# Feed-forwards that multiply both parts of x in one 512-column product, and run their down projections last

## The chip, the cores and the metric

The kernel runs on one core of a Trainium2 chip. The metric is device time of one launch in microseconds (us). A core has engines that work side by side and wait for each other through semaphores: TensorE (PE, matrix products, with PEld for its weight loads), VectorE (DVE), ScalarE (ACT), GpSimd (POOL), and SyncE (SP), which issues most DMAs. Each engine takes its own instructions strictly in the order in which the program gives them.

## The reference

Three blocks run one after another on x of 256 tokens by 1024 features, in fp32. The first mixes and then runs a mixture of 16 experts, the second runs a recurrence beside an attention, and the third, twice over, a feed-forward, an attention and another feed-forward. The change touches the five dense feed-forwards:

```python
# second block (d_ff 3072), once
xn = _rmsnorm(x, ffn_norm[l]); up = xn @ w_up[l]
g_ffn = _causal_dwconv(up[..., :D_FF], ffn_conv_w[l], ffn_conv_b[l])      # 3 taps along the tokens
x = x + (jax.nn.gelu(g_ffn) * up[..., D_FF:]) @ w_down[l]
# third block (d_ff 2816), four times
g, u = jnp.split(rmsnorm(x, norm) @ w_gu, 2, axis=-1)
x = x + 0.5 * ((jax.nn.silu(g) * u) @ w_down)
...
return rmsnorm(x, final_norm)
```

`rmsnorm(x, g)` is x times the inverse root of the mean square of a token, times the gain g of a feature.

## The kernel before

x is kept transposed in SBUF (`kn.xT`: feature in the partitions, eight blocks k of 128 features, 256 tokens along the free axis). Every weight matrix is cut into **units** of 256 output columns by up to eight blocks of 128 rows. `Stream` (L66 and after) holds six slots of 16 KB a partition. A raw chunk of two units lands in one slot by DMA from SP's queue; a unit is then split into two fp32r parts, hi by an ACT copy (`prep_one`, L221, recorded at L231) and lo = raw - hi by a DVE subtraction (`settle`, L236, recorded at L240). `take` (L252) hands a unit to the products and calls `ahead` (L244), which lets ACT split the unit two places further on. So in the step of unit n, ACT gets the hi copy of unit n+2 at the step's beginning and DVE gets its lo subtraction at the step's end.

A product of a unit with x is worked out from the parts: `lin_fm` (L348) issues, for each of two halves f of the unit's columns and each block k, three matmuls of 256 columns into one accumulator: hi weights by hi x, hi weights by lo x, lo weights by hi x. All products of all stages are recorded at L321. Each accumulator is one of eight PSUM banks of 512 fp32, taken in a ring; a unit uses one bank.

`step` (L411) writes down a unit's turn in this order: the products; if a norm is still open, `settle` and one piece of the norm (`pe_step`, L525); then one slice of every evacuation that was open before (`advance`, L388); `settle`; one slice of every background job. An evacuation is a generator: of a gate and up pair p, its first slice comes one step after the up product, the next slices in the steps after that.

A feed-forward (`plan_ffn` L1200, `ffn` L1224) goes over pairs p of a gate and an up unit, in groups g of four pairs (1024 hidden features; the last group has three pairs when d_ff is 2816). The order is: all pairs of group 0, all of group 1, the four down units of group 0, all of group 2, the downs of group 1, the downs of group 2. The four down units j of a group add into four banks `acc` that are held over all groups; after the last group each is added to xT, split anew for the next stage (`Next.pair`, two blocks k at once), and squared for the next norm (`Norm.pair`).

x enters the products unnormalized, only times the gain (`xgh`, `xgl`). The norm's factor of a token (`rb`, a tile of 128x256) comes during the first steps: after the first unit's products TensorE sums the squares (`nps`), DVE and POOL take the root, and after the second unit's products TensorE spreads it and ACT copies it (`rps`, `rb` at L521). The evacuation of a pair multiplies gate and up by `rb` while it reads PSUM: in `swiglu` (L1851) two DVE instructions at L1862 and L1864, a Silu on ACT (L1865), in the next step the product of the two on POOL (L1867), in the step after that the split into `hh` on ACT (L1247) and `hl` on DVE (L1248). In `ffn_two` (L1732) a convolution lies between: DVE L1744, L1746, ACT L1749, then DVE L1754 four times and ACT L1755, then POOL L1757.

At the very end `Last.finish` (L2392) multiplies xT by the final gain (ACT, L2396, eight instructions), makes the norm's factor, and `dump` (L2430) transposes on TensorE and writes out with ACT and SP.

Of the kernel before, what the change touches and what calls it, by code (L numbers as in the profile page):

```python
# [286 lines left out]
class Kern:  # L287
# [60 lines left out]
    def lin_fm(self, w, x, ps, start=True, stop=True, fs=(0, 1), cut=None):  # L348


        wh, wl = w
        xh, xl = x
        nk = wh.shape[1]
        whole = cut is None and stop
        for k0, k1 in self.cuts(nk, cut):
            for f in fs:
                o = ps[:, f * 256:(f + 1) * 256]
                c = slice(f * P, (f + 1) * P)
                if self.fine and cut is None and f == 1 and nk == 8:
                    self.tick()  # L360
                for k in range(k0, k1):
                    self.mm(o, wh[:, k, c], xh[:, k, :], start and k == 0 and (f == fs[0] or whole), False)
                    self.mm(o, wh[:, k, c], xl[:, k, :], False, False)
                    self.mm(o, wl[:, k, c], xh[:, k, :], False, stop and k == nk - 1)

# [102 lines left out]
class Norm:  # L468
# [3 lines left out]
    def __init__(self, kn, gain=None, late=False):  # L472
        self.kn, self.gain, self.late, self.last = kn, gain, late, None
        self.acc = kn.fx.tile([P, 512], F32, name="nacc", tag="nacc", bufs=2)
        self.n = 0
        self.state = 0

    def pair(self, x2):
        kn = self.kn
        sq = self.acc if self.n == 0 else kn.fx.tile([P, 512], F32, name="nsq", tag="nsq", bufs=1)  # L480
        if self.gain is None:
            kn.SC.activation(sq, x2, AF.Square)
        else:
            for f in range(2):
                kn.SC.activation(sq[:, f * 256:(f + 1) * 256], x2[:, f * 256:(f + 1) * 256], AF.Square, scale=self.gain(2 * self.n + f))
        if self.n == 3 and self.late:
            self.last = sq
        elif self.n:
            kn.G.tensor_tensor(self.acc, self.acc, sq, op=OP.add)  # L489
        self.n += 1  # L490

    def mean(self):
        kn = self.kn
        ps = kn.psB("nps")
        for t in range(2):
# [29 lines left out]
    def pe_step(self):  # L525
        if self.state == 0:
            self.columns()
        elif self.state == 1:
            self.rows()
            self.kn.norm = None  # L530
        self.state += 1
# [8 lines left out]


# [50 lines left out]

class Next:


    def __init__(self, kn, gain, norm=None, at=None):
        self.kn, self.gain = kn, gain
        self.hi, self.lo = (kn.act("xgh"), kn.act("xgl")) if at is None else (at[:, 0], at[:, 1])
        self.norm = norm or Norm(kn)

    def pair(self, j):
        kn = self.kn
        for k in (2 * j, 2 * j + 1):
            kn.split(self.hi[:, k, :], self.lo[:, k, :], kn.xT[:, k, :], self.gain(k))
        self.norm.pair(flat(kn.xT[:, 2 * j:2 * j + 2, :]))

# [617 lines left out]
def ffn(kn, plan, nx, gated, add, nxt, lend=0):  # L1224
# [4 lines left out]
    follow = None  # L1229
    for it in plan["order"]:  # L1230
        if it[0] in ("gate", "up"):
            _, p, u = it
            g, q = divmod(p, 4)
            ps = kn.psB(it[0])
            w = st.take(u)
            if it[0] == "gate":
                cur["g"] = ps
                kn.step(lambda: kn.lin_fm(w, nx.x, ps, cut=(2, 4, 6) if p == 0 else None))
            else:
                if q == 0:  # L1240
                    hs[g] = (kn.act("hh"), kn.act("hl")) if g != 1 else (kn.act2("hh"), kn.act2("hl"))

                def evac(p=p, q=q, g=g, pg=cur["g"], pu=ps):
                    o = slice(2 * q, 2 * q + 2)
                    t = yield from gated(p, pg, pu)
                    yield
                    kn.SC.activation(hs[g][0][:, o, :], t, AF.Copy)  # L1247
                    kn.V.tensor_tensor(hs[g][1][:, o, :], t, hs[g][0][:, o, :], op=OP.subtract)  # L1248
                kn.step(lambda: kn.lin_fm(w, nx.x, ps), evac)
        else:  # L1250
            _, g, j, u = it
            if g == last - 1 and j == 0:
                st.slots -= lend
            if acc is None:
                acc = [kn.psA("acc") for _ in range(4)]
            if g == last and j == 0:
                kn.flush()
                follow = nxt()
            w = st.take(u)
            n = sizes[g]  # L1260
            x = (hs[g][0][:, :n], hs[g][1][:, :n])

            def evac(j=j):
                add(j, acc[j])
                follow.pair(j)
            kn.step(lambda: kn.lin_fm(w, x, acc[j], start=g == 0, stop=g == last), evac if g == last else None, now=g == last and j == 3)
# [94 lines left out]
def mixer_two(kn, nx):  # L1361
# [3 lines left out]
    with ExitStack() as ctx:  # L1365
# [347 lines left out]
        follow = Next(kn, lambda k: kn.col("ffn_norm_2", k))  # L1713
# [18 lines left out]
def ffn_two(kn, nx):  # L1732
    V, SC, G = kn.V, kn.SC, kn.G
    with ExitStack() as ctx:
        kn.open_act2(ctx)
        pool = ctx.enter_context(kn.pool("ffn2"))
        kn.norm = nx.norm
        p3 = lambda ps: ps.rearrange("p (a b) -> p a b", a=2)

        def gated(p, pg, pu):  # L1740
            rb2 = nx.norm.rb2
            g = pool.tile([P, 2, 258], F32, name="g", tag="g", bufs=2)
            V.memset(g[:, :, 0:2], 0.0)
            V.tensor_tensor(g[:, :, 2:258], p3(pg), rb2, op=OP.mult)  # L1744
            tu = pool.tile([P, 2, S], F32, name="tu", tag="tu", bufs=3)
            V.tensor_tensor(tu, p3(pu), rb2, op=OP.mult)  # L1746
# [13 lines left out]
        def add(j, ps):  # L1760
            o = flat(kn.xT[:, 2 * j:2 * j + 2, :])
            V.tensor_tensor(o, ps, o, op=OP.add)

        return ffn(kn, kn.ffn2, nx, gated, add, lambda: Next(kn, lambda k: kn.col("ple_norm_2", k)))
# [86 lines left out]
def swiglu(kn, plan, nx, nxt, lend=0):  # L1851
    V, SC, G = kn.V, kn.SC, kn.G
    with ExitStack() as ctx:
        kn.open_act2(ctx)
        pool = ctx.enter_context(kn.pool("ffn3"))
        kn.norm = nx.norm
        p3 = lambda ps: ps.rearrange("p (a b) -> p a b", a=2)

        def gated(p, pg, pu):
            rb2 = nx.norm.rb2  # L1860
            t = pool.tile([P, 2, S], F32, name="t", tag="t", bufs=3)
            V.tensor_tensor(t, p3(pg), rb2, op=OP.mult)  # L1862
            tu = pool.tile([P, 2, S], F32, name="tu", tag="tu", bufs=3)
            V.tensor_tensor(tu, p3(pu), rb2, op=OP.mult)  # L1864
            SC.activation(t, t, AF.Silu)  # L1865
            yield
# [3 lines left out]
        def add(j, ps):  # L1870
            o = flat(kn.xT[:, 2 * j:2 * j + 2, :])
            V.scalar_tensor_tensor(o, ps, 0.5, o, op0=OP.mult, op1=OP.add)

        return ffn(kn, plan, nx, gated, add, nxt, lend)


def mixer_three(kn, nx, i):
# [4 lines left out]
    with ExitStack() as ctx:  # L1882
# [464 lines left out]
        for j in range(4):  # L2347
            until("out", 2 * j + 2)
            if j == 3:
                follow = Next(kn, lambda k: kn.col("ffn2_norm_3", 8 * i + k))  # L2350
# [30 lines left out]
class Last:  # L2381


    def __init__(self, kn):
        self.kn = kn
        self.norm = Norm(kn, late=True)
# [4 lines left out]

    def finish(self):  # L2392
# [5 lines left out]
        dump(kn, self.norm.rc)  # L2398


def block_three(kn, nx):
    for i in range(2):
        nx = swiglu(kn, kn.u3["f1", i], nx, lambda: Next(kn, lambda k: kn.col("mix_norm_3", 8 * i + k)), 1 - i)
# [3 lines left out]
                    (lambda: Next(kn, lambda k: kn.col("ffn1_norm_3", 8 + k))) if i == 0 else (lambda: Last(kn)))  # L2407
# [22 lines left out]
def dump(kn, rc=None):  # L2430

    kn.V.tensor_copy(kn.xT[:, 0, 0:1], kn.xT[:, 0, 0:1])
    with kn.pool("dump") as pool:
        o = kn.out.rearrange("b (t p) d -> p (b t) d", p=P)
        y = pool.tile([P, 2, D], F32, name="yo")
        for t in range(2):
            for q in range(2):
# [3 lines left out]
                if rc is None:  # L2441
                    kn.SC.activation(y[:, t, q * 512:(q + 1) * 512], ps, AF.Copy)
                else:
                    kn.SC.activation(y[:, t, q * 512:(q + 1) * 512], ps, AF.Copy, scale=rc[:, t:t + 1])
# [3 lines left out]
def build(tc, A, out, stages=(1, "e", 2, 3)):  # L2448
    with ExitStack() as ctx:
# [27 lines left out]
        if 2 in stages:  # L2477
# [44 lines left out]
```

## Time and profile before

| | us |
|---|---|
| median of 3 runs (2717.88 to 2722.27) | 2720.84 |
| the profiled execution's own time | 2721.21 |
| its span, first to last instruction | 2719.4 |
| PE busy in the span, 17617 matmuls | 2300.4 (85%) |
| DVE busy | 1130.3 (42%) |
| ACT busy | 911.1 (34%) |
| POOL busy | 355.4 (13%) |
| mean granted TensorE clock | 0.927 of full |

The profiled execution lies 0.37 us above the median. Shares are means over very different stages: the first 1340 us or so hold the first block and its experts and the recurrence, and the five feed-forwards lie in the second half of the span. Times below count from the span's start. A matmul's duration in a row is longer than the distance to the next one, as matmuls overlap in TensorE's pipeline: what it costs in a stream is the distance between starts. An idle time in square brackets is that of the engine before this instruction, with what ended it.

### The profile page before, as it was taken

To read this page: it belongs to the slowest core of one execution; us is meant where nothing else is said; L and a number is where in the kernel's file an instruction comes from. 1 tells how busy PE (TensorE), PEld (TensorE's weight loads), DVE (VectorE), ACT (ScalarE), POOL (GpSimd) and SP (SyncE) were. 2 spreads that over 40 slices of the span, in tenths; PEclk is the share of its full clock that TensorE was granted. 3 is DMA by queue.
4 is the path that set the end of the run, shared out by engine and by line. 5 is a ranking of instruction groups with operands and counts; after the bars stand their busy time and mean duration, and the time that the engine had idled before them with its cause. 6 is when DMAs were issued, how large, how long until landed. Compare 5 with 4: busy or idle time off the path is not lost. (4 is left out here: it accounts for less than half of the span.)

```text
span 2719.4 us, 39924 instructions
## 1 busy us (share of the span) xinstructions
PE 2300.4 (85%) x17617; PEld 1836.1 (68%) x17617; DVE 1130.3 (42%) x1325; ACT 911.1 (34%) x1223; POOL 355.4 (13%) x223
## 2 busy tenths in 40 slices
PE   7998766555566556589899999999999999998999
PEld 5987221111121111169899999999979999997998
DVE  5445000000000000049866666555686555558653
ACT  4343000000000000036845545434555444445533
POOL 0001000000000000002301212212322222130211
PEclk8998887887888787889999999999999999999999
DMA  8688999999999999984346555555335555562651
GB/s 325 232 279 346 389 428 427 428 428 428 428 428 428 428 427 428 428 301 152 132 155 221 186 186 171 186 179 177 94 96 185 187 192 175 180 173 78 201 186 63
DMA packets 266258, 717.92 MB, mean 264 GB/s; under 512 B 10995, under 2 KB 190436, under 8 KB 238436
## 3 DMA queue, kind: packets, MB, share of 16 engines
q1 hardware_dynamic: 262252, 710.38, 69.2%
q10 hardware_dynamic: 3000, 3.02, 0.5%
q8 instruction: 138, 2.26, 0.3%
q0 software_dynamic: 832, 1.97, 0.3%
q14 instruction: 36, 0.29, 0.0%
HBM read 713.89 MB, written 1.44 MB: 263 GB/s over the span
## 5 line engine op out<-in xcount | busy, mean ns | idle before, releaser
L240 DVE TENSOR_TENSOR w<-raw,w 128x2048 fp32r<-128x2048 f32 (+1 forms) x273 | 617.3, 2264 | 261.3 <-ACT w L231 261.2
L231 ACT ACTIVATE w<-raw 128x2048 fp32r<-128x2048 f32 (+1 forms) x273 | 510.9, 1875 | 568.5 <-PE up L321 137.7
L321 PE MATMUL gu<-raw,xe 128*32 128x512 f32 x1360 | 236.8, 833 | 175.9 <-DMA raw<-in_w_gate_e_dram 89.3
L321 PE MATMUL gate<-xgh,w 128*128 128x256 f32 x1792 | 329.0, 282 | 0.0
L321 PE MATMUL up<-xgh,w 128*128 128x256 f32 x1792 | 328.9, 282 | 0.0
L321 PE MATMUL acc<-hh,w 128*128 128x256 f32 x1792 | 320.6, 281 | 0.0
L321 PEld LDWEIGHTS gu<-raw,xe 128*32 128x32 f32 x1360 | 45.6, 132 | 362.9 <-issue 137.9
L321 PEld LDWEIGHTS up<-xgh,w 128*128 128x128 f32 x1792 | 278.9, 188 | 0.3 <-DVE w L240 0.2
L321 PEld LDWEIGHTS gate<-xgh,w 128*128 128x128 f32 x1792 | 278.9, 188 | 0.0
L321 PEld LDWEIGHTS acc<-hh,w 128*128 128x128 f32 x1792 | 275.6, 188 | 0.0
L321 PE MATMUL gate<-xgl,w 128*128 128x256 f32 x896 | 253.1, 282 | 4.4 <-DVE xgl L339 4.3
L1162 DVE TENSOR_TENSOR sg<-sg,gu 128x512 f32<-128x512 f32 x16 | 11.0, 688 | 583.3 <-PE gu L321 583.3
L321 PE MATMUL acc<-hl,w 128*128 128x256 f32 x896 | 252.1, 281 | 0.0
L321 PE MATMUL up<-xgl,w 128*128 128x256 f32 x896 | 252.1, 281 | 0.0
L1867 POOL TENSOR_TENSOR t<-t,tu 128x512 f32<-128x512 f32 x44 | 130.4, 2964 | 452.6 <-ACT t L1865 448.1
L321 PE MATMUL gu<-rawx,xe 128*32 128x512 f32 x688 | 109.0, 763 | 77.3 <-DMA rawx<-in_w_up_e_dram 41.2
L321 PEld LDWEIGHTS gate<-xgl,w 128*128 128x128 f32 x896 | 168.7, 188 | 5.9 <-DVE xgl L339 5.9
L321 PEld LDWEIGHTS acc<-hl,w 128*128 128x128 f32 x896 | 168.7, 188 | 0.0
L321 PEld LDWEIGHTS up<-xgl,w 128*128 128x128 f32 x896 | 168.7, 188 | 0.0
L321 PE MATMUL py<-raw,hT 128*32 128x512 f32 x672 | 93.5, 689 | 59.5 <-DMA raw<-in_w_down_e_dram 51.4
L321 PEld LDWEIGHTS gu<-rawx,xe 128*32 128x32 f32 x688 | 21.5, 124 | 168.2 <-issue 53.2
L1170 ACT ACTIVATE hT<-ph 128x512 f32<-128x512 f32 x16 | 9.6, 597 | 359.1 <-PE ph L1168 359.1
(441 smaller groups left out, 3366.9 us busy)
## 6 DMA issues: line engine op xcount, KB each, us to landing
raw<-in_w_up_e_dram SPq DMA_DIRECT2D x44, 2048.0 KB, 39.1
raw<-in_ffn_w_gu_dram SPq DMA_DIRECT2D x88, 1024.0 KB, 6.6
raw<-in_w_down_e_dram SPq DMA_DIRECT2D x42, 2048.0 KB, 39.1
raw<-in_w_gate_e_dram SPq DMA_DIRECT2D x41, 2048.0 KB, 39.1
rawx<-in_w_gate_e_dram SPq DMA_DIRECT2D x23, 2048.0 KB, 39.1
rawx<-in_w_down_e_dram SPq DMA_DIRECT2D x22, 2048.0 KB, 39.1
rawx<-in_w_up_e_dram SPq DMA_DIRECT2D x20, 2048.0 KB, 39.1
raw<-in_w_in_dram SPq DMA_DIRECT2D x32, 1024.0 KB, 9.1
```

The lines of the kernel that those rows point to most:

```text
L231: kn.nc.scalar.activation(wh, v, AF.Copy)
L240: self.kn.nc.vector.tensor_tensor(wl, v, wh, op=OP.subtract)
L321: self.nc.tensor.matmul(out, lhsT, rhs, start=start, stop=stop, skip_group_check=True)
L1162: V.tensor_tensor(sg, sg, pu, op=OP.mult)
L1170: SC.activation(flat(hT), ph, AF.Copy)
L1867: G.tensor_tensor(t, t, tu, op=OP.mult)
```

## The change

1. **One product for both parts.** x's parts lie side by side in tiles of four blocks (`Parts`), so that hi and lo of a block are one operand of two strips of 256 columns. `lin_both` replaces `lin_fm` in the feed-forwards: per f and k one matmul of 512 columns (hi weights by hi x and lo x, into the two halves of a bank) and one of 256 (lo weights by hi x, into the first half). A half f of a unit now fills a bank of its own.
2. **The halves are summed at evacuation.** `join` sums the two halves of each bank with a DVE tensor_reduce over pairs that lie 256 apart.
3. **x is scaled by the norm as well.** A background job `Scaled` makes, in four slices, a second pair of parts of x that holds gain and `rb`; pairs from p = 4 on use it and skip the multiplication by `rb`. Pairs 0 to 3 use the unscaled x as before, and multiply by `rb` in SBUF after `join`.
4. **Downs behind all gates and ups**, j by j over the groups, with two accumulator banks for one j; each j is added to xT when its last group is done, and the last unit is split into its two halves, each followed by its own addition, split and square.
5. **Norms.** `fold=True` sums the squares to 256 columns before TensorE sees them (half the `nps` matmuls) and makes the norm begin one step later; `wants` leaves out the unused `rps` and `rb` of the attentions' norms.
6. **The end.** The final gain becomes a diagonal matrix in a TensorE product that also transposes; DVE and ACT share the output's evacuation, and it is written in four DMAs on two queues.

```diff
+    def join(self, out, pss):
+        for f, ps in enumerate(pss):
+            self.V.tensor_reduce(out[:, f, :], ps.rearrange("p (h s) -> p s h", h=2), axis=AX.X, op=OP.add)
+    def lin_both(self, w, x, ps, start=True, stop=True, fs=(0, 1), cut=None):
...
+        for k0, k1 in self.cuts(nk, cut):
+            for f in fs:
+                o = ps[f].rearrange("p (h s) -> p h s", h=2)
+                c = slice(f * P, (f + 1) * P)
+                for k in range(k0, k1):
+                    self.mm(o, wh[:, k, c], x.both(k), start and k == 0, False)
+                    self.mm(o[:, 0, :], wl[:, k, c], x.hi[:, k, :], False, stop and k == nk - 1)
 class Norm:
-        self.state = 0
+        self.state = -1 if fold else 0
...
     def plan_ffn:
-    ups(0)
-    for g in range(1, len(sizes)):
+    for g in range(len(sizes)):
         ups(g)
-        downs(g - 1)
-    downs(len(sizes) - 1)
+    for j in range(4):
+        for g in range(len(sizes)):
+            order.append(("down", g, j, st.linear(ph, Wd, 8 * g, sizes[g], j * 256)))
+class Scaled:
+    def run(self, kn, nx, pool):
+        while not hasattr(nx.norm, "rb"):
+            yield
+        for q in range(4):
+            tmp = pool.tile([P, 2, S], F32, name="xs", tag="xs", bufs=2)
+            for f in range(2):
+                k = 2 * q + f
+                kn.V.scalar_tensor_tensor(tmp[:, f, :], kn.xT[:, k, :], nx.gain(k), nx.norm.rb, op0=OP.mult, op1=OP.mult)
+            o = slice(2 * q, 2 * q + 2)
+            kn.SC.activation(self.parts.hi[:, o, :], tmp, AF.Copy)
+            yield
+            kn.V.tensor_tensor(self.parts.lo[:, o, :], tmp, self.parts.hi[:, o, :], op=OP.subtract)
+        self.ready = 1
 def ffn(...):
+            x = nx.parts if p < 4 else xs.parts
+            ps = [kn.psB(it[0]) for _ in range(2)]
...
+            def half(f):
+                kn.lin_both(w, hs[g], acc, start=False, fs=(f,))
+                if f == 0:
+                    kn.advance(len(kn.late))
+                    st.settle()
+                add(6 + f, acc[f])
+                follow.part(6 + f)
 def swiglu: gated(p, pg, pu, scaled):
             t = pool.tile([P, 2, S], F32, name="t", tag="t", bufs=3)
-            V.tensor_tensor(t, p3(pg), rb2, op=OP.mult)
+            kn.join(t, pg)
+            if not scaled:
+                V.tensor_tensor(t, t, nx.norm.rb2, op=OP.mult)
+            SC.activation(t, t, AF.Silu)
-            V.tensor_tensor(tu, p3(pu), rb2, op=OP.mult)
-            SC.activation(t, t, AF.Silu)
+            kn.join(tu, pu)
+            if not scaled:
+                V.tensor_tensor(tu, tu, nx.norm.rb2, op=OP.mult)
 class Last: finish
-        for k in range(8):
-            kn.SC.activation(kn.xT[:, k, :], kn.xT[:, k, :], AF.Copy, scale=kn.col("final_norm_3", k))
+            kn.mm(pss[q, t][:, (k % 4) * P:(k % 4 + 1) * P], kn.xT[:, k, t * P:(t + 1) * P], self.diag[:, k, :], True, True)
```

`ffn_two` gets the same treatment: join gate, join up, then the two multiplications by `rb` for p below 4, then the convolution as before.

## Rows read from the trace of the kernel before

**Rows 1.** Windows, the feed-forwards: stretch, length, engines' busy time (instructions), granted clock, DMA share, GB/s
```profile
1450.18:1657.01 206.83, 206.83 (x1747) 206.83 (x1745) 130.38 (x145) 103.99 (x111) 38.97 (x18) 1.00 0.54 180
...
2516.49:2707.24 190.75, 190.10 (x1598) 189.53 (x1597) 101.07 (x77) 80.00 (x66) 42.04 (x17) 1.00 0.46 153
sum 971.28, PE 966.78 PEld 964.84 DVE 545.29 ACT 436.56 POOL 206.40; mean PE 193.36 PEld 192.97 DVE 109.06 ACT 87.31 POOL 41.28
```

**Rows 2.** Page, costliest groups: shape, count, busy us, mean ns, idle before
```profile
L321 PE MATMUL gate<-xgh,w 128*128 128x256 f32 x1792 | 329.0, 282 | 0.0
L321 PE MATMUL gate<-xgl,w 128*128 128x256 f32 x896 | 253.1, 282 | 4.4 <-DVE xgl L339 4.3
```

**Rows 3.** Timeline of PE in a down unit: start us, us, engine, line, op
```profile
1800.28 0.28 PE L321 MATMUL acc<-hl,w 128*128 128x256 f32 x1
...
1803.84 0.28 PE L321 MATMUL acc<-hl,w 128*128 128x256 f32 x1
```

**Rows 4.** Timeline of PE where 512 and 256 columns alternate, an attention
```profile
2001.47 0.28 PE L321 MATMUL S<-mask,identr 128*128 128x256 f32 x1
...
2001.59 0.63 PE L321 MATMUL S<-keys,QS 128*128 128x512 f32 x2
...
2002.05 0.28 PE L321 MATMUL S<-mask,identr 128*128 128x256 f32 x1
```

**Rows 5.** Timeline of PE, six matmuls of 512 columns in a row, first block
```profile
59.56 1.55 PE L321 MATMUL tps<-csr,uf 128*128 128x512 f32 x6
60.95 0.28 PE L321 MATMUL psA<-hh,w 128*128 128x256 f32 x1
```

**Rows 6.** Timeline of DVE around one evacuation, third block
```profile
2194.86 0.69 DVE L1248 TENSOR_TENSOR hl<-t,hh 128x512 fp32r<-128x512 f32 x1 [2.92 <-ACT hh L1247]
2195.47 0.69 DVE L1862 TENSOR_TENSOR t<-gate,rb 128x512 f32<-128x512 f32 x1
2196.07 0.68 DVE L1864 TENSOR_TENSOR tu<-up,rb 128x512 f32<-128x512 f32 x1
2196.66 2.28 DVE L240 TENSOR_TENSOR w<-raw,w 128x2048 fp32r<-128x2048 f32 x1
...
2221.41 0.89 DVE L339 SCALAR_TENSOR_TENSOR xgl<-xT,PT,xgh 128x256 fp32r<-128x256 f32 x2 [1.27 <-ACT xgh L338]
```

**Rows 7.** Timeline of ACT around the same evacuation
```profile
2192.39 1.92 ACT L231 ACTIVATE w<-raw 128x2048 fp32r<-128x2048 f32 x1 [2.78 <-PE up L321]
2194.21 0.61 ACT L1247 ACTIVATE hh<-t 128x512 fp32r<-128x512 f32 x1
2196.18 0.64 ACT L1865 ACTIVATE t<-t 128x512 f32<-128x512 f32 x1 [1.36 <-DVE t L1862]
```

**Rows 8.** Groups of DVE by shape, 1686 to 2708 us: a reduction from PSUM
```profile
L2193 DVE TENSOR_REDUCE nm<-S 128x2 f32<-128x512 f32 x16 | 10.3, 681 | 1.6 <-PE S L321 1.6
```

**Rows 9.** Timeline of DVE in the second block's feed-forward
```profile
1467.55 1.92 DVE L1754 SCALAR_TENSOR_TENSOR t<-g,PT,t 128x256 f32<-128x256 f32 x4
```

**Rows 10.** Timelines of PE and ACT: a norm's sums, and the copy of rb
```profile
2237.99 1.05 PE L321 MATMUL nps<-ones,nacc 128*128 128x1 f32 x8
...
1463.11 0.39 ACT L521 ACTIVATE rb<-rps 128x256 f32<-128x256 f32 x1 [5.12 <-PE rps L321]
```

**Rows 11.** Timeline of PE, a long wait in an attention
```profile
1898.70 0.58 PE L321 MATMUL un<-w,xgh 128*128 128x256 f32 x1 [3.80 <-DVE w L240]
```

**Rows 12.** Windows in the attentions: after waits of 3.8, 2 and 4.2 us; clock behind the counts
```profile
1898.28:1901.69 3.41, 2.99 (x14) 2.99 (x15) 2.79 (x4) 1.94 (x2) 0.95 (x1) 0.50 0.00 0
...
1940.20:1942.00 1.80, 1.80 (x15) 1.80 (x16) 1.77 (x3) 1.80 (x2) 0.00 (x0) 1.00 0.35 59
...
2461.48:2468.31 6.83, 4.38 (x19) 4.00 (x20) 6.22 (x17) 2.52 (x10) 0.00 (x0) 0.50 0.00 0
```

**Rows 13.** Timeline of the end, 2704 to 2720 us
```profile
2708.76 3.29 ACT L2396 ACTIVATE xT<-xT,PT 128x256 f32<-128x256 f32 x8
...
2710.82 3.52 PE L2440 MATMUL ops<-ident,xT 128*128 128x128 f32 x16 [0.42 <-DVE xT L2432]
```

More of the change, by code (lines that the diff above doesn't have):

```diff
@@ L494, in mean @@
         ps = kn.psB("nps")
+        if self.fold:
+            for i, a in enumerate((self.acc, self.last) if self.late else (self.acc,)):
+                for t in range(2):
+                    kn.mm(ps[:, t:t + 1], a[:, t * P:(t + 1) * P], kn.ones[:, 0:1], i == 0 and t == 0, i == self.late)
+            return ps[:, 0:2]
         for t in range(2):
@@ L527, in pe_step @@
             self.columns()
+            if "r" not in self.wants:
+                self.kn.norm = None
         elif self.state == 1:
@@ L538 @@
 class TwoNorms(Norm):
+    wants = "cr"
     def __init__(self, kn, g1, sums):
@@ L590, in rows, with __init__, __getitem__, both @@
         kn.bgs.append(scale())
+class Part:
+    def __init__(self, tiles, n, h):
+        self.tiles, self.n, self.h = tiles, n, h
+    def __getitem__(self, at):
+        p, k, c = at
+        if isinstance(k, slice):
+            k0, m = k.start, k.stop - k.start
+            return self.tiles[k0 // self.n][p, self.h, k0 % self.n:k0 % self.n + m, c]
+        return self.tiles[k // self.n][p, self.h, k % self.n, c]
+class Parts:
+    def __init__(self, kn, act, name, m=2):
+        self.n = 4
+        self.tiles = [a(name).rearrange("p (h k) s -> p h k s", h=2) for a in (act if isinstance(act, tuple) else (act,) * m)]
+        self.hi, self.lo = (Part(self.tiles, 4, h) for h in range(2))
+    def both(self, k):
+        return self.tiles[k // 4][:, :, k % 4, :]
 class Next:
@@ L605, in pair, with part @@
         self.norm.pair(flat(kn.xT[:, 2 * j:2 * j + 2, :]))
+    def part(self, k):
+        kn = self.kn
+        kn.split(self.hi[:, k, :], self.lo[:, k, :], kn.xT[:, k, :], self.gain(k))
+        if self.norm.fold:
+            self.norm.part(kn.xT[:, k, :], k % 2)
+        elif k % 2:
+            self.norm.pair(flat(kn.xT[:, k - 1:k + 1, :]))
     @property
@@ L1229, in ffn @@
     follow = None
+    xs = Scaled(kn, nx, pool)
+    kn.bgs.append(xs.gen)
     for it in plan["order"]:
@@ L1233, in ffn @@
             g, q = divmod(p, 4)
-            ps = kn.psB(it[0])
+            if p == 4 and it[0] == "gate":
+                kn.drain(xs.gen)
+                assert xs.ready
+            x = nx.parts if p < 4 else xs.parts
+            ps = [kn.psB(it[0]) for _ in range(2)]
             w = st.take(u)
@@ L1258, in ffn, with evac @@
                 follow = nxt()
+            if g == 0:
+                acc = [kn.psA("acc") for _ in range(2)]
             w = st.take(u)
[L1260 to L1264, printed above, removed]
+            def evac(j=j, acc=acc):
+                for f in range(2):
+                    add(2 * j + f, acc[f])
                 follow.pair(j)
-            kn.step(lambda: kn.lin_fm(w, x, acc[j], start=g == 0, stop=g == last), evac if g == last else None, now=g == last and j == 3)
+            def half(f):
+                kn.lin_both(w, hs[g], acc, start=False, fs=(f,))
+                if f == 0:
+                    kn.advance(len(kn.late))
+                    st.settle()
+                add(6 + f, acc[f])
+                follow.part(6 + f)
+            if g == last and j == 3:
+                kn.step(lambda: [half(f) for f in range(2)])
+            else:
+                kn.step(lambda: kn.lin_both(w, hs[g], acc, start=g == 0, stop=g == last), evac if g == last else None)
     kn.flush()
@@ L2385, in __init__ @@
         self.kn = kn
-        self.norm = Norm(kn, late=True)
+        self.norm = Norm(kn, late=True, fold=True)
+        self.diag = kn.act("diag", F32).rearrange("p a s -> p (a s)")[:, 0:8 * P].rearrange("p (k n) -> p k n", k=8)
+        for k in range(8):
+            kn.SC.activation(self.diag[:, k, :], kn.ident, AF.Copy, scale=kn.col("final_norm_3", k))
     def pair(self, j):
@@ L2390, in pair, with part @@
         self.norm.pair(flat(kn.xT[:, 2 * j:2 * j + 2, :]))
+    def part(self, k):
+        self.norm.part(self.kn.xT[:, k, :], k % 2)
     def finish(self):
```

132 lines of the change are left out of this document (86 added, 46 removed).

## The prediction, on record before the result

> **What bounds the kernel now.** I read the windows of the five feed-forwards first, then the groups of PE, then the timelines of DVE and ACT. In the windows the reader is to see that TensorE is busy in 967 of 971 us at full clock, while DVE works 545 and ACT 437, and that the DMA engines are about half busy [rows 1]. So the feed-forwards go at TensorE's rate, and a product of three matmuls is the thing to price. Gate, up and acc have 1792 + 896 matmuls each [rows 2], three names: 8064 matmuls, 2688 triples. Ten triples take 1803.84 - 1800.28 = 3.56 us [rows 3], 356 ns each, 118.7 ns a matmul; a unit of 16 triples takes 5.70 us.
>
> **The product.** A triple of 3 x 256 columns becomes a 512 and a 256: the same 768 columns, two instructions. Where 512s and 256s alternate, the 256 takes 0.12 us and two 512s take 2002.05 - 2001.59 = 0.46, 230 ns each [rows 4]; six 512s in a row take 1.39, 232 each [rows 5]. I take 231 + 119 = 350: 6 ns less for a triple, 2688 x 6 = **-16 us**. Bounds: the two strips of the operand might cost as two matmuls (356, no gain); if all above 256 columns at 2.4 GHz (106.7 ns) were a price per instruction, 12 ns, the 512 would take 225 and the gain be 32. I stay with the rows that show a 512.
>
> The Trainium skill (TensorE: Matmul & The Clock Gate, "Back-to-back issue gap") has a rule that speaks against the change: a warm matmul costs its columns at 2.4 GHz plus about 2.5 ns. By it a joined instruction would give 2.5 ns, 2688 x 2.5 = 7 us, and the forecast would be 9 us higher. The rows disagree with its level (119 where it has 109, 231 where it has 216), but agree that columns, not instructions, are most of the price.
>
> **What DVE and ACT get in the first four pairs.** This is where I see the price. Prices, start to start in a full queue, from [rows 6]: `hl` 0.6, a multiplication by `rb` 0.6, lo of a weight unit 2.2, a 256-column scalar_tensor_tensor 0.4. From [rows 7]: hi of a weight unit 1.9, `hh` 0.6. A reduction of 128x512 from PSUM takes 0.68 [rows 8] like the multiplication beside it, so 0.6 in a queue, and a `join` of one unit 1.2; no row shows pairs that lie 256 apart, so bounds: 0.6 (256 outputs as a 256-wide instruction) and 2.4 for a unit, taken 1.2, the same elements read. Evacuating a pair costs DVE 1.2 + 0.6 + 1.2 + 0.6 = 3.6 for p below 4 where it was 1.2, and 2.4 after. A slice of `Scaled` costs 0.8 on DVE, 0.6 on ACT, then 0.6 on DVE in the next step.
>
> Only order matters now. In a step ACT's queue has hi of unit n+2, then evacuation, then Scaled's hi; DVE's has evacuation, lo of n+2, then Scaled. But Scaled's hi waits for DVE's last instruction of its step, and the next step's weight hi stands behind it; DVE's lo waits for that hi, and before it `hl` waits for `hh`, which stands behind the hi too. The two engines take turns instead of overlapping. I follow a `swiglu` from its first matmul, unit = 16 x 350 = 5.6 us:
>
> - `fold` opens the norm one step later: `nps` after unit 1, `rps` after unit 2. Unit 2 ends at 3 x 5.6 + 0.45 = 17.2; with `rps` (some 0.4, an estimate) and the copy of 0.39 [rows 10] `rb` is there at 18.0. DVE has joined gate 0 and stands at the multiplication. Then 0.6 + 1.2 + 0.6 + 0.8 (Scaled 0) = 21.2.
> - Step 3: Scaled's hi 0.6, weight hi 1.9, weight lo 2.2, Scaled 1.4: 27.3.
> - Step 4: 0.6, 1.9, `hh` 0.6, `hl` 0.6, evacuation 3.6, weight lo 2.2: 36.8 is when unit 6 can start; TensorE was ready at 6 x 5.6 + 0.8 = 34.4. Then Scaled 1.4: 38.2.
> - Step 5: 6.1: 44.3.
> - Step 6: 0.6 + 1.9 + 0.6 + 0.6 + 3.6 + 2.2 = 9.5: lo of unit 8 at 53.8; TensorE was ready at 8 x 5.6 + 0.8 = 45.6.
>
> So a `swiglu` loses 8.2 us by its ninth unit, 2.4 before unit 6 and nearly all the rest before unit 8, x 4 = **+33**. From p = 4 on, an evacuation step has 0.3 + 1.9 + 0.6 + 0.6 + 2.4 + 2.2 = 8.0 us before its lo is done, of 11.2 until it is wanted: no wait. Bounds of a `swiglu`: nothing, since DVE's own work in that chain is 24.6 us of the 27.6 between `rb` and unit 8; and 8.2 + 6 with joins of 2.4 (five joins of a unit lie behind `rb`).
>
> In `ffn_two` both joins stand ahead of the multiplications, so less is left when `rb` comes, and the convolution (four of 0.4 [rows 9]) falls into the steps without a join. Followed the same way: `rb` 18.0; two multiplications and Scaled 0, 20.1; step 3, weight hi behind Scaled's and lo: 25.0, Scaled 26.4; step 4, evacuation 3.6 and lo: 32.2, Scaled 33.6; step 5, Scaled's hi, weight hi, `hh`, `hl`, convolution 1.6, lo: 41.2 against 40.0 when unit 7 is wanted; Scaled and the split of `pT`, 43.2; step 6, evacuation and lo 49.1, step 7 `xl` 49.7. Unit 8 waits till then, against 45.6: **+3.5**; with joins of 2.4 about 14.
>
> **The clock.** Unit 8 of a `swiglu` comes after 5 us of idle. In an attention TensorE waited 3.80 us [rows 11], and the granted clock was 0.50 from 1898.28 to 1901.69, with 2.99 us of matmuls in it; around 2461.48 another long wait has 6.83 us at 0.50 with 4.38 of matmuls; after a wait of 2 us the clock stayed 1.00 [rows 12]. Half of such matmul time is lost, 1.5 to 2.2; I take 2 x 4 = **+8**, bounds 0 and 14.
>
> **The rest.** Five folded norms issue 4 for 8 `nps` (1.05 us for 8, [rows 10]): -2.5; two attentions' `rps` and `rb` go, some -0.5. **-3**, bounds 0 and -5. The end loses ACT's scaling of xT 3.29 (partly behind the norm) and, of the 16 transposes 3.52 that lay on the path [rows 13], all but what now runs while the root is taken: **-2.5**, bounds 0 and -5. The downs' move keeps instructions and bytes; SP issues loads of 256 instead of 512 columns for some of them, hidden by DMA engines that are half idle [rows 1], and if that cover went, a late unit would cost TensorE its own wait, which I put at 0 to +5. Four additions where one was (0.69 to 4 x 0.4 for a j) fall on steps of down units where DVE has no evacuation. POOL's queue loses some norm work; ACT's `diag` (eight small copies) lies in down steps.
>
> **Sum**, against the profiled execution's own 2721.2 (2719.4 of span and 1.8 around it): 2721.2 - 16 - 3 - 2.5 + 33 + 3.5 + 8 = 2744.2. That execution is 0.4 above the median; I say **2744**.
>
> **Rivals.**
> 1. *The queues keep up.* Then nothing but the gains is left: 2721.2 - 21.5 = 2700. For it: DVE is busy 56% and ACT 45% of the feed-forwards now, and the lo is made two units ahead. Against it: the ping-pong needs no full engine, only order, and it is in both queues' order. It decides at 27.6 us for the chain; I count 35.8. Chance 0.20.
> 2. *The pair sums are slow*, 2.4 for a unit: 14.2 x 4 + 14 in place of 33 + 3.5, 2744 + 34 = 2778. For it: an access pattern that no row shows; against: every row of DVE from PSUM goes by elements. Chance 0.10.
> 3. *Instructions, not columns, cost*: gain 32, chain about 3 longer over the five: 2744 - 16 + 3 = 2731. Against: [rows 4, 5]. Chance 0.07.
> 4. *Half of each wait is absorbed* (weight units a little further ahead, no clock loss), so that gain and loss cancel: about 2721. Chance 0.06.
>
> The forecast has 0.57, with its own range 2725 to 2768. Fewer instructions that save nothing would be its upper part, 2760.
>
> **The numbers.** A measurement of this kernel tells a change from none at about 0.2%, 5.4 us. Faster: rival 1 and part of 4, 0.22. Within: 0.05. Slower: 0.73. The range holds the forecast, rival 1 to its lower third and rival 2: 2696 to 2780.
>
> **What will show it.** Waits of PE before unit 6 and unit 8 of each `swiglu`, ended by DVE's lo of a weight unit, with DVE waiting for ACT's hi just before, and stretches at 0.50 clock behind them; 2688 matmuls of 512 columns at a distance of some 231 ns; no waits in the pairs from p = 4 on and in the downs. If TensorE runs through units 2 to 8 with no gap, the chain is wrong and rival 1 is right; if joins last over 1 us each, rival 2; if a triple is under 345 ns, rival 3.

## The result, and the profile after

The changed kernel takes 2767.34 us (median of 4 runs, 2763.51 to 2769.80) against 2720.17 for the kernel before on the same chip (4 runs, 2717.88 to 2722.27): ratio 1.0171, 95% interval 1.0159 to 1.0183. It is slower by 47 us; 24 were forecast. The profiled execution took 2763.51, with a span of 2761.7, so the traces differ by 42.3 in span.

Windows over the same five feed-forwards as [rows 1], kernel after (stretch, length, busy time of PE, PEld, DVE, ACT, POOL with their instructions, granted clock, DMA share, GB/s):

```profile
1446.70:1658.69 211.99, 205.87 (x1167) 180.05 (x1166) 161.09 (x201) 106.91 (x117) 42.54 (x20) 0.99 0.54 175
1689.87:1892.92 203.05, 191.06 (x1064) 165.95 (x1065) 147.53 (x142) 88.19 (x82) 45.12 (x19) 0.98 0.51 167
2054.15:2256.48 202.33, 192.02 (x1066) 166.60 (x1065) 137.72 (x135) 88.04 (x78) 44.31 (x20) 0.97 0.54 174
2256.48:2455.52 199.04, 190.16 (x1067) 166.08 (x1066) 132.38 (x135) 83.93 (x74) 40.39 (x16) 0.98 0.54 172
2550.42:2752.64 202.22, 191.60 (x1067) 166.01 (x1066) 139.48 (x130) 84.70 (x80) 43.58 (x21) 0.97 0.45 144
sum 1018.63, PE 970.71 PEld 844.68 DVE 718.20 ACT 451.78 POOL 215.94; mean PE 194.14 PEld 168.94 DVE 143.64 ACT 90.36 POOL 43.19
```

The five lengths sum to 1018.6 where they were 971.3: +47.4, more than the 42.3 by which the spans differ (the table near the end has the rest). TensorE idled 4.5 us in them before and 47.9 now, and the clock is below 1.00 in all five, where it was 1.00. After the last product the end is shorter: 2752.64 to 2761.7, 9.1 us, against 12.2 between [rows 1] and the span before.

Is the product itself cheaper? The page's groups that answer to [rows 2], and the timeline of PE that answers to [rows 3] (start us, us, engine, line, op), the third `swiglu`:

```profile
L327 PE MATMUL acc<-h,w 128*128 128x512 f32 (+1 forms) x1792 | 315.7, 339 | 2.1 <-DVE h L1364 2.1
L327 PE MATMUL gate<-xn,w 128*128 128x512 f32 (+1 forms) x1152 | 218.5, 348 | 22.9 <-DVE w L240 22.3
```

```profile
2285.46 5.78 PE L327 MATMUL up<-xg,w 128*128 128x512 f32 x32
2291.07 0.39 PE L327 MATMUL gate<-xg,w 128*128 128x512 f32 x1
2295.30 4.96 PE L327 MATMUL gate<-xg,w 128*128 128x256 f32 x18 [3.84 <-DVE w L240]
```

It is: a unit of 32 matmuls goes from 2285.46 to 2291.07, 5.61 us, 351 ns a pair against 356 a triple. The last row is the cost: unit 6 has one matmul, and then TensorE waits 3.84 us for DVE's lo of a weight unit. DVE ahead of it, and ahead of unit 8 (answering to [rows 6]):

```profile
2274.84 0.69 DVE L1989 TENSOR_TENSOR t<-t,rb 128x512 f32<-128x512 f32 x1 [1.48 <-ACT rb L564]
...
2277.38 1.92 DVE L1325 SCALAR_TENSOR_TENSOR xs<-xT,PT,rb 128x256 f32<-128x256 f32 x2
2281.79 2.29 DVE L240 TENSOR_TENSOR w<-raw,w 128x2048 fp32r<-128x2048 f32 x1 [2.50 <-ACT w L231]
2284.00 0.69 DVE L1329 TENSOR_TENSOR xn<-xs,xn 128x512 fp32r<-128x512 f32 x1
2284.61 0.87 DVE L1325 SCALAR_TENSOR_TENSOR xs<-xT,PT,rb 128x256 f32<-128x256 f32 x2
2288.50 0.69 DVE L1364 TENSOR_TENSOR h<-t,h 128x512 fp32r<-128x512 f32 x1 [3.02 <-ACT h L1363]
...
2292.96 2.29 DVE L240 TENSOR_TENSOR w<-raw,w 128x2048 fp32r<-128x2048 f32 x1
2295.16 1.78 DVE L1329 TENSOR_TENSOR xn<-xs,xn 128x512 fp32r<-128x512 f32 x1
...
2300.22 2.29 DVE L240 TENSOR_TENSOR w<-raw,w 128x2048 fp32r<-128x2048 f32 x1 [2.49 <-ACT w L231]
...
2311.39 2.29 DVE L240 TENSOR_TENSOR w<-raw,w 128x2048 fp32r<-128x2048 f32 x1
```

And ACT over the same time (answering to [rows 7]):

```profile
2274.43 0.38 ACT L564 ACTIVATE rb<-rps 128x256 f32<-128x256 f32 x1 [4.59 <-PE rps L327]
...
2279.32 0.63 ACT L1327 ACTIVATE xn<-xs 128x512 fp32r<-128x512 f32 x1 [3.12 <-DVE xs L1325]
2279.86 1.90 ACT L231 ACTIVATE w<-raw 128x2048 fp32r<-128x2048 f32 x1
2285.51 0.63 ACT L1327 ACTIVATE xn<-xs 128x512 fp32r<-128x512 f32 x1 [3.75 <-DVE xs L1325]
2286.05 1.90 ACT L231 ACTIVATE w<-raw 128x2048 fp32r<-128x2048 f32 x1
2287.85 0.61 ACT L1363 ACTIVATE h<-t 128x512 fp32r<-128x512 f32 x1
```

Read them together. DVE ends `xs`; ACT, which waited 3.12 us for it, copies it (`xn`, 2279.32) and only then makes the weight's hi; DVE, which waited 2.50 us for that hi, makes the lo and the next `xs`; ACT waited 3.75 for that. Each engine is idle while the other works: the turn-taking of the forecast, with its waits in the places it named. Windows at the two late units' restarts show the clock (the third number from the right is the granted clock: 0.50, the level of 1.2 GHz):

```profile
2296.51:2299.92 3.41, 3.41 (x13) 2.93 (x12) 1.22 (x3) 2.16 (x2) 0.00 (x0) 0.50 0.00 0
2313.57:2316.99 3.42, 3.26 (x10) 2.88 (x11) 3.42 (x3) 2.43 (x2) 1.24 (x1) 0.50 0.00 0
```

Each `swiglu` has two half-speed stretches, beside TensorE's waits for units 6 and 8. Most last 3.4 us; the one at unit 8 lasts 6.8 in the second and the last `swiglu` (2112.15 to 2119.01, 2607.12 to 2613.95). `ffn_two` has one of 3.4, from 1497.8, beside a wait of 2.41 us for its unit 8.

### The profile page after: what moved, and what is told of

It reads as the page before. It is cut to its first block, busy times and chain, and to the rows that moved or that the text cites. A ratio compares the mean times of both kernels' runs of the same rounds, so it can differ in the third digit from the quotient of the medians.

```text
span 2761.7 us, 34925 instructions
## 1 busy us (share of the span) xinstructions
PE 2301.3 (83%) x14909; PEld 1712.6 (62%) x14909; DVE 1300.4 (47%) x1598; ACT 920.1 (33%) x1245; POOL 355.4 (13%) x235
## 3 DMA queue, kind: packets, MB, share of 16 engines
q8 instruction: 117, 1.92, 0.3%
## 4 chain that ended last, share of the span: by engine, by line
PE 37%; DVE 8%; ACT 3%; issue 2%; ACTq 0%; POOL 0%; DVEq 0%; POOLq 0%
PE acc L327 11%; PE gate L327 9%; PE up L327 8%; PE psA L327 3%; DVE w L240 3%; PE un L327 2%; ACT w L231 2%; PE wo L327 1%; DVE xs L1325 1%; DVE tu L319 1%; PE po L327 1%; DVE xg L345 1%; DVE xn L1329 1%; DVE t L319 0%; PE S L327 0%
## 5 line engine op out<-in xcount | busy, mean ns | idle before, releaser
L327 PE MATMUL acc<-h,w 128*128 128x512 f32 (+1 forms) x1792 | 315.7, 339 | 2.1 <-DVE h L1364 2.1
L327 PEld LDWEIGHTS acc<-h,w 128*128 128x128 f32 x1792 | 276.1, 188 | 40.8 <-DVE h L1364 2.4
L327 PE MATMUL gate<-xn,w 128*128 128x512 f32 (+1 forms) x1152 | 218.5, 348 | 22.9 <-DVE w L240 22.3
L327 PEld LDWEIGHTS gate<-xn,w 128*128 128x128 f32 x1152 | 184.3, 196 | 51.9 <-DVE w L240 24.5
L327 PE MATMUL up<-xn,w 128*128 128x512 f32 (+1 forms) x1152 | 208.1, 339 | 0.0
L327 PEld LDWEIGHTS up<-xn,w 128*128 128x128 f32 x1152 | 177.5, 188 | 24.8
L327 PE MATMUL gate<-xg,w 128*128 128x512 f32 (+1 forms) x640 | 125.4, 353 | 21.2 <-DVE w L240 15.3
L327 PE MATMUL psA<-xg,w 128*128 128x256 f32 x1104 | 141.4, 289 | 1.3 <-DVE w L240 0.8
L327 PEld LDWEIGHTS psA<-xg,w 128*128 128x128 f32 x1104 | 137.2, 193 | 3.3 <-issue 1.9
L327 PE MATMUL up<-xg,w 128*128 128x512 f32 (+1 forms) x640 | 117.5, 340 | 3.0 <-DVE w L240 3.0
```

The costliest lines, as they stand in the source:

```text
L327: self.nc.tensor.matmul(out, lhsT, rhs, start=start, stop=stop, skip_group_check=True)
```

## The experiments

All times below are medians against the kernel before on the same chip: 2718.67 us beside the first four runs, 2719.73 beside the next four, 2719.12 beside the last two. A difference from the kernel after is one between such sets, whose kernel before moved by up to 1.5 us.

### No scaled x

```
-    xs = Scaled(kn, nx, pool)
-    kn.bgs.append(xs.gen)
-            x = nx.parts if p < 4 else xs.parts
+            x = nx.parts
-                    t = yield from gated(p, pg, pu, p >= 4)
+                    t = yield from gated(p, pg, pu, False)
```

> The changed kernel without Scaled: all pairs use the unscaled x and multiply by rb in SBUF. Theory (ACT and DVE take turns because Scaled's slices stand between the weight units): the waits before units 6 and 8 of each feed-forward go, with the half clock behind them; the trace of the changed kernel has 12.8 us of them in a swiglu (units 6 to 8 take 11.24 + 6.06 + 12.32 instead of 3 x 5.62) and about 6.5 in ffn_two, so 2767 - 4 x 12.8 - 6 = 2710 (2703 to 2722), below the kernel before. Rival (DVE has too much to do altogether, for the doubled evacuation): DVE does 1.2 us more for each later pair, so the waits only spread over the later pairs, 2745 or more. Rival (the norm that comes a step later is the cause): a wait stays before units 6 and 8, 2730 or more.

Measured: 2735.12 us, ratio 1.0060 (1.0047 to 1.0072). The waits before units 6 and 8 are gone, and 32 us with them, but 25 more were expected. Windows of the first and the third `swiglu`, the waits of PE in the first (us in total, times, longest), and ACT's timeline in each:

```profile
1683.32:1887.31 203.99, 191.09 (x1065) 164.45 (x1066) 151.70 (x144) 85.43 (x78) 45.03 (x19) 0.99 0.51 166
...
2239.63:2426.96 187.33, 186.53 (x1067) 163.34 (x1065) 134.14 (x137) 81.87 (x70) 40.39 (x16) 1.00 0.57 182
```

```profile
PE gate L327 <- DVE w L240: 6.4, 7, 1.0
```

```profile
1749.20 1.92 ACT L231 ACTIVATE w<-raw 128x2048 fp32r<-128x2048 f32 x1 [4.97 <-DVE w L240]
...
1761.74 1.92 ACT L231 ACTIVATE w<-raw 128x2048 fp32r<-128x2048 f32 x1 [4.99 <-DVE w L240]
...
2294.96 3.85 ACT L231 ACTIVATE w<-raw 128x2048 fp32r<-128x2048 f32 x2 [3.55 <-DVE w L240]
...
2306.19 3.86 ACT L231 ACTIVATE w<-raw 128x2048 fp32r<-128x2048 f32 x2 [3.55 <-DVE w L240]
```

The same work settles in one of two rhythms. In the third `swiglu` a round takes 2306.19 - 2294.96 = 11.23 us, TensorE's own time for two units; in the first, 1761.74 - 1749.20 = 12.54, and TensorE waits at each gate. DVE and POOL in a slow round of the first `swiglu`, then in a fast one of the second:

```profile
1743.59 5.57 DVE L240 TENSOR_TENSOR w<-raw,w 128x2048 fp32r<-128x2048 f32 x2
1743.84 3.17 POOL L1991 TENSOR_TENSOR t<-t,tu 128x512 f32<-128x512 f32 x1 [9.36 <-DVE tu L1989]
...
2116.47 2.28 DVE L240 TENSOR_TENSOR w<-raw,w 128x2048 fp32r<-128x2048 f32 x1
2116.73 3.20 POOL L1991 TENSOR_TENSOR t<-t,tu 128x512 f32<-128x512 f32 x1 [8.05 <-DVE tu L1989]
```

In the slow rhythm DVE makes two lo right behind each other beside POOL's product and takes 5.57 us, where 2.2 + 2.3 = 4.5 would do: 1.1 of the 1.3 us by which the rounds differ (what POOL does to DVE comes below, with the product on DVE). In the fast one DVE waits for ACT between the two, and POOL is done by then. So multiplying every pair by `rb` costs too, once DVE and ACT stand in the wrong order; the expectation had priced only amounts. What makes a feed-forward fall into one rhythm or the other I did not trace.

### The copy one step later

`Scaled` issues the same instructions, but ACT's copy of a slice comes one step after its `xs`, and DVE's lo one step after that, so nobody waits within a step.

```
-        for q in range(4):
-            ...                           (xs of slice q)
-            kn.SC.activation(self.parts.hi[:, o, :], tmp, AF.Copy)
-            yield
-            kn.V.tensor_tensor(self.parts.lo[:, o, :], tmp, ...)
+        tmps = {}
+        for i in range(6):
+            if i >= 2:
+                ...                       (o, two blocks of slice i - 2)
+                kn.V.tensor_tensor(self.parts.lo[:, o, :], tmps[i - 2], ...)
+            if 1 <= i < 5:
+                kn.SC.activation(self.parts.hi[:, 2 * i - 2:2 * i, :], tmps[i - 1], AF.Copy)
+            if i < 4:
+                ...                       (xs of slice i, as before)
+            if i < 5:
+                yield
```

> The changed kernel with Scaled's work unchanged, but each slice's ACT copy given one step later, so that it stands behind the next weight unit's hi instead of ahead of it; its DVE subtraction comes another step later. Theory (order, not amount): the wait before unit 6 goes and unit 8 waits only for Scaled's last subtraction, 1 to 6 us in place of 9.4 and with at most one stretch at half clock: 2767 - 4 x 6 to 4 x 10 = 2727 to 2743. Rival (amount of DVE work in the first four pairs): the same instructions on the same engines, 2760 to 2770.

Measured: 2734.53 us, 1.0059 (1.0045 to 1.0072). Equal work in another order is 33 us faster, so order, not amount, made most of the loss. The wait before unit 6 goes; unit 8 is still late, now because its slice of x is made last (in the first and the last `swiglu` the lo of a weight unit is late by 2.2 us as well, and `ffn_two` waits 5.4 us for x). PE's waits in the third `swiglu`:

```profile
PE gate L327 <- DVE xn L1325: 2.5, 2, 2.4
```

### The norms unfolded

```
-  Norm(kn, wants="r", fold=True)
+  Norm(kn, wants="r")            (ahead of all five feed-forwards)
```

> The changed kernel with the five feed-forward norms not folded: 8 nps matmuls again, and the norm begins a step earlier, so that rb is there about 6 us earlier in units. Theory: the chain of Scaled's turns is as long, but starts earlier; followed through the queues it loses 4 us less in a swiglu and the wait before unit 8 shrinks to 1 to 2 us, which also saves one stretch at half clock: 2767 - 4 x (4 + 1.7) + 2.2 = 2746 (2735 to 2755). Rival (the late norm is the whole cause): no wait left, 2715. Rival (amount of DVE work): the work is the same but has one step more, a small gain, 2755 to 2765.

Measured: 2744.14 us, 1.0093 (1.0080 to 1.0107): 23 us faster than the kernel after. `rb` comes one step earlier, the chain starts earlier. The fold, which I priced at a gain of 2.5, cost 23 here.

### The 512 columns given as two strips

```
-                    self.mm(o, wh[:, k, c], x.both(k), start and k == 0, False)
+                    self.mm(o[:, 0, :], wh[:, k, c], x.hi[:, k, :], start and k == 0, False)
+                    self.mm(o[:, 1, :], wh[:, k, c], x.lo[:, k, :], False, False)
```

> The changed kernel with each 512-column product given as its two strips of 256 columns, all else as it is: prices the joined product by itself. The changed kernel has 175.6 ns a matmul in pairs of 512 and 256 (351 ns a pair) against 356 for three of 256 before, 4.8 ns x 2688 = 13 us. Theory: 2767 + 13, less some 3 us as the waits shrink with longer units: 2777 (2772 to 2782). Rival (joining saves nothing, the lower distance comes from elsewhere): 2767.

Measured: 2777.88 us, 1.0216 (1.0202 to 1.0230), 10.5 above the kernel after: the joined product does gain, by about the 12.5 us that its shorter distance is worth.

### Both re-timings together

The later copy and the unfolded norms in one kernel.

> Both re-timings in one kernel: Scaled's copy and low part each one step later, and the five norms ahead of the feed-forwards unfolded, so that rb is there a step earlier. All the products are as in the kernel after. Theory (order: the scaled x is late because its start waits for rb and each of its links waits for a turn of the other engine): the wait before unit 8, about 10 to 12 us where 5.6 would do in the run with the later copy alone, goes, and with it its half-clock stretch: four swiglu stretches shorter by 4 to 5 us, ffn_two by about 5, against 2 for the separate root and columns: 2712 (2704 to 2722). Rival (amount: DVE can't do joined evacuation, weights and Scaled in the time of eight units): the late unit stays and the time is that of the later copy alone, 2734, or the two gains overlap and it is over 2728.

Measured: 2710.27 us, 0.9971 (0.9961 to 0.9982): 0.3% faster than the kernel before, with every product and pair sum of the changed kernel in it. The two gains add: 33 + 23 = 56 of 57. Windows of the first and third `swiglu`, and the sum over all five feed-forwards:

```profile
1687.80:1880.55 192.75, 187.99 (x1068) 163.82 (x1069) 146.38 (x142) 88.13 (x81) 47.51 (x17) 1.00 0.54 176
...
2231.35:2418.07 186.72, 186.72 (x1071) 163.81 (x1070) 132.66 (x135) 83.66 (x73) 42.05 (x15) 1.00 0.57 183
sum 964.93, PE 954.25 PEld 834.10 DVE 716.67 ACT 450.69 POOL 223.06; mean PE 190.85 PEld 166.82 DVE 143.33 ACT 90.14 POOL 44.61
```

In the third, TensorE is busy in all of its 186.72 us while DVE does the same 133 us of work as in the kernel after. DVE and ACT where the copy and lo now stand:

```profile
2266.29 0.89 DVE L1332 SCALAR_TENSOR_TENSOR xs<-xT,PT,rb 128x256 f32<-128x256 f32 x2
2267.09 2.29 DVE L240 TENSOR_TENSOR w<-raw,w 128x2048 fp32r<-128x2048 f32 x1
2269.29 0.69 DVE L1325 TENSOR_TENSOR xn<-xs,xn 128x512 fp32r<-128x512 f32 x1
2270.20 0.69 DVE L1369 TENSOR_TENSOR h<-t,h 128x512 fp32r<-128x512 f32 x1 [0.22 <-ACT h L1368]
```

```profile
2261.00 0.62 ACT L1327 ACTIVATE xn<-xs 128x512 fp32r<-128x512 f32 x1
2264.64 1.92 ACT L231 ACTIVATE w<-raw 128x2048 fp32r<-128x2048 f32 x1 [3.02 <-issue]
```

ACT's copy has no wait ahead of it, and DVE's `h` waits 0.22 us for ACT where it waited 3.02.

### Half the price of a pair sum

`join` copies the high strip alone; the product of the weights' high part with x's low part is left out of the result.

```
-            self.V.tensor_reduce(out[:, f, :], ps.rearrange("p (h s) -> p s h", h=2), axis=AX.X, op=OP.add)
+            self.V.tensor_copy(out[:, f, :], ps[:, 0:256])
```

> The evacuation takes the high strip of the 512-column product alone (the product of the weights' high part with x's low part is left out of the result), so that each evacuation of a gate or up costs DVE about half of 0.68 us; the order of everything else is as in the kernel after. Theory (order, turns of DVE and ACT): the chain before units 6 and 8 only loses the part of it that stands behind evacuations, 2.5 to 3.5 us per swiglu: 2753 (2747 to 2758), and the waits before units 6 and 8 stay. Rival (the price of the pair sum is the cause): the waits go, 8 to 11 us per swiglu and ffn_two: 2705 to 2720.

Measured: 2753.37 us, 1.0128 (1.0114 to 1.0142). A copy takes 414 ns where the sum takes 681, and 14 of 47 us go with that, as counted. The late units stay: 2.2 and 4.1 us of wait before units 6 and 8 of each `swiglu` (and 1.4 before unit 7 of three), where it was 3.8 and 4.9.

### No scaled x and half the price

Both edits above (the same part left out).

> No scaled x (all pairs take the unscaled one and are multiplied by rb) and the evacuation of the high strip alone (the product of the weights' high part with x's low part is left out). Theory: what was left in the kernel without scaled x, gates of 6.9 us where 5.6 would do in two of the four swiglus, is DVE's doubled evacuation, and it goes: 2710 (2704 to 2718). Rival (those gates wait for ACT's high weights, whatever DVE's evacuation costs): as without scaled x alone, 2731 to 2737.

Measured: 2706.67 us, 0.9953 (0.9940 to 0.9967). PE's waits in the first `swiglu`:

```profile
PE gate L327 <- DVE xg L345: 4.0, 3, 1.4
```

The waits for weights at every gate are gone; what is left is the feed-forward's start. So the slow rhythm of the kernel without scaled x went when DVE had 1.1 us less of evacuation per pair (four sums of 681 ns made copies of 414). The two lo beside POOL's product take 5.58 us here too (at 1753.44), so the blocked lo alone doesn't make the gates late; it adds to the evacuation in one round. Whether taking the block away instead (no scaled x, and POOL's product on DVE) would do as well was not tried.

### The product on DVE

The product of silu and up of pairs 0 to 3 of the four `swiglu` moves from POOL to DVE.

```
-            G.tensor_tensor(t, t, tu, op=OP.mult)
+            (G if scaled else V).tensor_tensor(t, t, tu, op=OP.mult)
```

> The product silu times up of pairs 0 to 3 of the four swiglus is done on DVE and no longer on POOL; all else as in the kernel after. Theory (DVE's operations are slowed while POOL's product runs, which is the part of the chain that the prediction had too small): Scaled's operations fall from up to 1.9 us to 0.7 to 0.9, the chain is shorter by 1 to 2 us per swiglu net of the product's own 0.7 to 1.3 us on DVE: 2761 (2755 to 2766). Rival (the slow rows have another cause, such as their operands): their durations stay, and the product only adds to DVE: 2767 to 2776.

Measured: 2756.17 us, 1.0138 (1.0124 to 1.0151): giving DVE more work makes the kernel 11 us faster (9 by the two ratios; the two profiled executions differ by 7.8, of which 6.6 lie in the feed-forwards). TensorE's waits before units 6 and 8 fall from 8.7 us to 7.1 or 7.7 in a `swiglu`. The reason is in the timelines. POOL in the kernel after:

```profile
2277.60 1.41 POOL L1996 TENSOR_TENSOR t<-t,tu 128x512 f32<-128x512 f32 x1 [8.13 <-DVE tu L1994]
...
2293.18 3.20 POOL L1996 TENSOR_TENSOR t<-t,tu 128x512 f32<-128x512 f32 x1 [14.18 <-DVE tu L1994]
```

Beside the first, DVE's two `xs` took 1.92 us where two later took 0.87. The second began while DVE made a weight's lo (2292.96 to 2295.25), lasted 3.20, and DVE's next `xn` (2295.16) took 1.78 instead of 0.69, ending half a microsecond after POOL. The Trainium skill (SBUF — State Buffer, "Who interferes with whom") states this: a DVE instruction with two SBUF inputs contends with a GpSimd instruction that reads SBUF, and the one issued second blocks. The trace agrees: 2.29 + 1.41 - 0.22 (POOL's later start) is 3.48, near the 3.20.

Groups of DVE's pair sums and its instructions of `Scaled`, feed-forwards to the end, first in the kernel after, then with the product on DVE (count | busy us, mean ns):

```profile
L319 DVE TENSOR_REDUCE tu<-up 128x256 f32<-128x512 f32 x112 | 71.6, 681 | 0.0
...
L1329 DVE TENSOR_TENSOR xn<-xs,xn 128x512 fp32r<-128x512 f32 x20 | 22.9, 1143 | 0.0
L1325 DVE SCALAR_TENSOR_TENSOR xs<-xT,PT,rb 128x256 f32<-128x256 f32 x40 | 22.7, 607 | 0.0
```

```profile
L1325 DVE SCALAR_TENSOR_TENSOR xs<-xT,PT,rb 128x256 f32<-128x256 f32 x40 | 18.5, 503 | 0.0
...
L1329 DVE TENSOR_TENSOR xn<-xs,xn 128x512 fp32r<-128x512 f32 x20 | 14.2, 708 | 0.0
```

### All three, and the product of ffn_two too

The first run has the later copy, the unfolded norms and the product of the four `swiglu` on DVE; the second has the product of `ffn_two`'s pairs 0 to 3 there as well.

> The later copy and the unfolded norms together, and the product silu times up of pairs 0 to 3 of the four swiglus on DVE. Theory: with both re-timings only the first and the last swiglu still wait (gates of units 6 and 8 of 6.6 and 7.5 us where the others take 5.6, about 3 us each, of which DVE's operations of 1.8 us beside POOL's product are the larger part); these go, nothing else changes: 2706 (2702 to 2710). Rival (the two swiglus wait for something else, as the first weights that come late after the attention, or DVE loses as much by the products as it gains): 2709 to 2714.

Measured: 2708.09 us, 0.9961 (0.9949 to 0.9974). The first and the last `swiglu` are 1.3 us shorter each; half of what they waited stays (one gate takes 7.04 us in one, 7.05 in the other), so the theory holds for half of the amount it named. The late gates are those of units 8 and 10, not 6 and 8 as the expectation has it. The median alone doesn't tell this kernel from the one with both re-timings (2710.27): the two intervals overlap.

> As the run before, and the product gelu times up of pairs 0 to 3 of ffn_two on DVE too. Theory: ffn_two has no late scaled x left in this order (all its gates and ups take 5.6 us), so nothing is gained there: as the run before, within 2 us. Rival (the products on DVE come in the way of its evacuations): ffn_two longer by 2 us or more.

Measured: 2707.24 us, 0.9958 (0.9944 to 0.9971): no difference, `ffn_two` 206.4 us in both. These two have the lowest medians of those that leave nothing out: 11 to 12 us under the kernel before, 60 under the kernel after.

## Why the prediction was right, and where its sizes were off

The direction and the mechanism were right, and the time lies within the range, though only just within the forecast's own (2725 to 2768); the sum was 23 us short. Its steps:

| Step | Forecast, us | Shown, us | By |
|---|---|---|---|
| 512-column product | -16 | -12.5 | PE busy 966.8 before, 954.3 in the kernel with both re-timings |
| chain in 4 `swiglu` and `ffn_two` | +36.5 | +39.0 | PE's waits before units 6 and 8 (in `ffn_two` 7 and 8) |
| other waits of TensorE | 0 | +4.4 | PE idle 4.5 and 47.9, less the row above |
| clock | +8 | +16 to +19 | half of some 31 us of matmuls at 0.50; PE busy 970.7 after, 951.8 with neither scaled x nor full sums, at 1.00 |
| end | -2.5 | -3.1 | last product to end of span |
| fewer norm instructions | -3 | about -2.5 | PE busy 954.3 re-timed (unfolded), 951.8 (folded) |

The rest of the 42.3 us between the spans is +1.5 between the feed-forwards and -3.5 ahead of the first, whose start lies between 1445.8 and 1450.3 us in the traces of all these kernels. The largest part of the miss is the clock.

*The product.* 4.7 ns saved per joined pair x 2688 = 12.5, not 6 x 2688. It stands between the forecast's value and the 2.5 ns per instruction that the prediction weighed (7 us) from the Trainium skill (TensorE: Matmul & The Clock Gate, "Back-to-back issue gap"). Rival 3, a price per instruction of 12 ns, is out.

*The pair sums.* 681 ns for a 128x512 read as pairs 256 apart, as taken from [rows 8]; rival 2 is out.

*The chain.* Where it breaks was named in advance: before units 6 and 8, and behind them nothing but 0.26 us in one `swiglu`. Rival 4 (half of each wait absorbed) is out with it. The waits came near the forecast, 3.84 + 4.89 = 8.7 us a `swiglu` for 8.2, but that is in part luck, for the chain itself was mis-sized. Unit 6 went on at 2295.30 - 2256.48 = 38.8 us after the `swiglu`'s start where 36.8 was forecast, and the lo of unit 8 ended at 57.2 (2311.39 + 2.29) where 53.8 was. TensorE came to unit 8 some 2 us later too, as units 6 and 7 ran in part at half speed (13.1 us from unit 6's restart to unit 8's first matmul at 2308.37, where two units take 11.2), and so waited less there. The term that failed is the price of `Scaled` on DVE, taken as 0.8 for two `xs` and 0.6 for a lo; beside POOL's product they took 1.92 and 1.78, where 0.87 and 0.69 are the rows without it: 2.1 of the 3.4 us. I had taken both prices from rows where POOL was quiet, and had not asked what POOL does while they run. The trace of the kernel before had the sign, in the shortest, median and longest time of POOL's product (ns):

```profile
L1867 POOL TENSOR_TENSOR t<-t,tu x44: 1289/3147/3207, 1708.5 to 2672.2; 128x512 f32<-128x512 f32 x44
```

Moving the product gave 11 us back. In `ffn_two` the waits were 1.64 and 2.41; the prediction's own steps give 49.7 - 45.6 = 4.1 there, though it put 3.5 into its sum.

*The clock.* I counted one half-speed stretch per `swiglu`, since the wait before unit 6 was forecast as 2.4 us, and [rows 12] show the clock staying up after a wait given as 2, which is 1.72 in the trace (at 1940.16). The wait became 3.84, and a stretch at 0.50 stood there too; two of the stretches at unit 8 were twice as long. Nor would 2.4 us have been safe: `ffn_two` has a stretch beside its wait of 2.41, and with the product on DVE, where unit 6 waits 2.8, two of the four `swiglu` have one. The step that failed is the count of stretches, made between rows of 1.72 and 3.8 us with none in between.

*The fold.* The step "fewer norm instructions, -3" was right for what goes and looked at nothing else, though the chain I walked begins with `rb` one step later. Unfolding alone gives 23 us. Had I walked the chain with `rb` a step earlier, as the expectation of that run did (2746, measured 2744), the prediction would have said that one argument of `Norm` decides half the loss.

*Not foreseen:* in `ffn_two` the downs wait 2.1 us for the last `h` (in the page's acc group above). No gate or up is left to run behind the last pair, and its evacuation takes a step more than a `swiglu`'s; that this is the cause was not tested.

Rival 1 (the queues keep up, 2700) was wrong for this order and nearly right for another: with the order mended, the same products take 2707 to 2710.

## What to carry to other kernels

When a change gives two helper engines more work, busy shares (DVE went to 71% of the feed-forwards, ACT 44%) don't tell whether TensorE waits; walk each queue in order and look for a place where A waits for B's last instruction of a step while B's next waits for A. Such a loop is mended by issuing the dependent instruction one step later, with no work removed: here 33 us. And take a duration from a row in which the other engines do what they will do in the new kernel.

## What the hardware showed that I had not expected

- A DVE instruction with two inputs in SBUF and a POOL `tensor_tensor` stop each other: 0.69 becomes 1.78 us on DVE, 1.41 becomes 3.20 on POOL. Putting POOL's share on DVE cost DVE 0.68 a product and was faster here, by 11 us.
- The same instructions in the same queues settled in rounds of 11.23 or 12.54 us in one execution, depending on the feed-forward; in the slow rounds a weight's lo ran into POOL's product each time.
